# Paired heads, an output product by chunks, a token table by expert, and unread products on TensorE in an encoder layer

## The chip, the cores and the metric

The kernel runs on one core of a Trainium2 chip. The metric is device time of one execution in microseconds (us). Three executions of the kernel before took 1742.06, 1747.69 and 1747.76 us; their median is 1747.69 us. In the profile PE is the matrix engine (PEld its weight loads), DVE the vector engine, ACT the scalar engine, POOL the general engine that also issues indirect transfers, and SP the engine that issues most of the others.

## The reference

One encoder layer on 512 tokens of width 1024, all in float32, written for depth 1:

```python
proj = h @ w_in                      # A: q,k,v  B: q,k,v  C: q,k,v  and three gates
oa = windowed_gqa_sink(...)          # 8 heads, window of 128 each way, sink logit
ob = diff_attention(...)             # 4 heads, softmax1 - lam * softmax2
oc = neighbourhood_attention(...)    # 8 heads on an 8 x 64 grid
merged = sum(sigmoid(gate_i) * (branch_i @ w_branch_i))
x = layer_norm(alpha * x + merged @ w_out)
logits = x @ w_router + b_router     # top 4 of 32 experts, softmax over the 4
y = act(x @ w_up[e] + b_up[e]) @ w_down[e] + b_down[e]     # clamped SwiGLU
x = layer_norm(alpha * x + weighted sum of y over the token's experts)
```

The weights of the 32 experts are 32 x (1024 x 2048 + 1024 x 1024) floats, 384 MB in transfers of 1 MB.

## The kernel before

**Numbers.** A float32 operand is split into a rounded part (`whi`, `vh`, `ph`, suffix h) and a remainder (suffix l), both of the type fp32r, ACT making the first and DVE the second. A product is then three matmuls: h·h, l·h and h·l. Experts of the kind L are computed so for up to 128 tokens, experts of the kind S in plain float32 for up to 64, in the order of the string `KINDS` (16 of each, L and S mostly in turn).

**Attention.** `proj` (L126) makes a projection for 128 columns in 24 matmuls. `banded` (L230) does one head of A or C: for each of four blocks of 128 queries `scores` (L198) makes two matmuls, L203 over 128 rows (both parts of q against the rounded k) and L204 over the head's 64 rows (the remainder of k), and `soft` (L207) adds the bias, finds the maximum and takes the exponential into a tile `E`. Then the probabilities are turned on PE (L260), split (`split_pt`) and multiplied with v by `pv3` (L225): L226 `vh·ph`, L227 `vl·ph`, L228 `vh·pl`, each with 64 output rows. The two heads of a pair are done one after the other. `att_b` does the same for B with 512 keys per block and 128 output rows. `Fill` takes the next projections and the gated branch products (`ph2_items`) as filler between these steps. A list scheduler then sets the order on each engine.

**The middle.** After the last branch product, `w_out` comes in eight chunks of 512 KB (L792), is split (L793, L794), and `out_product` (L778) makes the output product: for the token chunks c = 0, 1, 2 together, k by k, then for c = 3. `layer_norm1` (L723) follows for each chunk: residual sum (L729), turning on PE (L737), statistics, router logits (L748), the top four and the mask `M`. After c = 3 come the positions of all tokens in their experts (L816 to L823), a one-hot of expert 0's tokens and the gathering of their rows on PE (L835, four chunks), the split of these rows (`xt0`), and `finish1` of all four chunks, which writes X1 and Y.

**The experts.** `weights` (L1052) hands out the stream of 1 MB weight tiles. Eight tiles hold raw weights: `rawu` (four) and `rawv` (four), filled by SP (L610 up, L615 down) as they come free. An L tile comes free when ACT and DVE have split it (L1064, L1065) into a ring of three; an S tile when PE has used it. The first eight are expert 0's; whose weights come next is in `order`, which `sort` (L888) computes while `up(0)` (L1071) has begun. `table` (L910) writes a token's place into T in DRAM with 16 indirect transfers on POOL (L933), in the sorted order of the experts, and reads the table back; `pick` (L1019) on POOL copies the columns that put an expert's bias on PE. Expert 1, of the kind S, starts with `pick` and `gather_small`. From expert 6 on `overflow` tests once whether any expert has too many tokens.

Of the kernel before, what the change touches and what calls it, by code (L numbers as in the profile page):

```python
# [23 lines left out]
P = 128  # L24
S = 512
# [18 lines left out]
def kernel_body(ctx, tc, a, out, dbg=None, cap=128):  # L44
# [56 lines left out]
    for k in range(8):  # L101
        t = att.tile([P, NB, P], F32, name="E", bufs=7) if k < 7 else att.tile([P, NB, P], F32, name="t", bufs=3)
# [66 lines left out]
    def make_v(w, permuted, box):  # L169
# [8 lines left out]
        vh = att.tile([P, NB, P], F32R, name="vh", bufs=2)  # L178
        vl = att.tile([P, NB, P], F32R, name="vl", bufs=2)
# [3 lines left out]
        nc.scalar.copy(vh, pt)  # L183
        nc.vector.tensor_sub(vl, pt, vh.bitcast(F32))
        box["v"] = (vh, vl)
# [12 lines left out]
    def scores(box, u, qb, ks, ke):  # L198
        q2, (k2, kl) = box["q"], box["k"]
        r = slice(u * 64, u * 64 + 64)  # L200
        qs = slice(qb * P, qb * P + P)
        ps = ps_s.tile([P, S], F32, name="sc")
        nc.tensor.matmul(ps[:, :ke - ks], q2[:, u, qs], k2[:, u, ks:ke], start=True, stop=False)  # L203
        nc.tensor.matmul(ps[:, :ke - ks], q2[r, u, qs], kl[r, ks:ke], start=False, stop=True)  # L204
        return ps[:, :ke - ks]

    def soft(ps, bias, n, init, mcol, scol):  # L207
# [3 lines left out]
        e = att.tile([P, S], F32, name="E", bufs=7)  # L211
# [18 lines left out]
    def banded(box, u, biasf, init, sinkc, done):  # L230
        vh, vl = box["v"]
        vc = slice(u * 64, u * 64 + 64)
        m = att.tile([P, NB], F32, name="m", bufs=4)
        s = att.tile([P, NB], F32, name="s", bufs=4)
        es = []
        for qb in range(NB):
            ks, ke = rng(qb)
            ps = scores(box, u, qb, ks, ke)
            es.append(soft(ps, biasf(qb), ke - ks, init, m[:, qb:qb + 1], s[:, qb:qb + 1]))
            yield  # L240
        if sinkc is not None:
            sk = att.tile([P, NB], F32, name="sk", bufs=2)
            nc.scalar.activation(sk, m, AF.Exp, bias=sinkc)
            nc.vector.tensor_add(s, s, sk)
        r = att.tile([P, NB], F32, name="r", bufs=4)
        nc.vector.reciprocal(r, s)
        for qb in range(NB):
            ks, ke = rng(qb)
            nc.vector.tensor_scalar(es[qb][:, :ke - ks], es[qb][:, :ke - ks], r[:, qb:qb + 1], None,
                                    op0=ALU.mult)  # L250
        yield
        po = ps_o.tile([P, S], F32, name="o")
        pend = None
        for i, kb in enumerate((1, 2, 0, 3)):
            qs = [qb for qb in range(NB) if abs(qb - kb) <= 1]
            pt = ps_t.tile([P, S], F32, name="pt")
            n = len(qs) * P
            for j, qb in enumerate(qs):
                c0 = kb * P - rng(qb)[0]
                nc.tensor.transpose(pt[:, j * P:(j + 1) * P], es[qb][:, c0:c0 + P], ident)  # L260
            ph, pl = split_pt(pt, n)
            if pend:
                pv3(*pend)
            pend = (po[:64, qs[0] * P:qs[0] * P + n], n, ph, pl, vh[:, kb, vc], vl[:, kb, vc], i == 0, i == 3)
            yield
        pv3(*pend)
        done(po[:64])
        yield
# [4 lines left out]
    def evac_o(po, br, half, permuted):  # L273
        bh, bl = br
        r = slice(half * 64, half * 64 + 64)
        hi, hf, lo, src = bh[r], bh[r].bitcast(F32), bl[r], po
        if permuted:
            hi, hf, lo = perm(hi), perm(hf), perm(lo)
            src = out4(src)
        if half == 0:  # L280
# [1219 lines left out]
```

## Time and profile before

| what | value |
|---|---|
| median of three executions | 1747.69 us |
| the profiled execution | 1744.16 us |
| its span (first to last instruction) | 1742.3 us |
| PE busy | 1611.0 us, 92% |
| DVE busy | 940.0 us, 54% |
| ACT busy | 778.3 us, 45% |
| POOL busy | 207.1 us, 12% |
| mean granted clock of PE | 0.975 of 2.4 GHz |
| read from DRAM | 466.78 MB, 278 GB/s over the span |

Busy time of PE counts a matmul from its start to a modelled end, and matmuls overlap, so a PE that is "busy" for a whole stretch can be streaming or only draining. How far apart the starts of two matmuls are says more. The granted clock of a stretch is given as a share of 2.4 GHz. The profile's page cuts the span into 40 slices: up to about 550 us PE is busy and the transfers are light (60 to 80 GB/s), from 700 us to 1714 us both are near full (about 400 GB/s), and between the two neither is.

### The profile page before, as it was taken

Reading aid. Unit: us, or ns where it says so; the run is one execution under the profiler, and the core shown is the slowest. Engines: PE = TensorE matmul, PEld = TensorE weight load, DVE = VectorE, ACT = ScalarE, POOL = GpSimd, SP = SyncE. Lnnn points to the kernel's source line nnn. Section 1 sums busy time; section 2 is a strip of 40 time slices with the busy share of each in tenths; the row PEclk is TensorE's granted clock in tenths of the full one; section 3 lists DMA queues with packets and bytes.
Section 4 is the critical chain, followed back from the end, with each engine's and each line's share of the span. In section 5 each row is a group of like instructions: output and inputs, shape, how many; then the busy total and the mean of one; then the engine's idle time right before and its main releaser. Section 6 shows DMA issues by size and latency. Waiting matters only on the chain.

```text
span 1742.3 us, 19860 instructions
## 1 busy us (share of the span) xinstructions
PE 1611.0 (92%) x7130; PEld 1053.7 (60%) x7130; DVE 940.0 (54%) x1340; ACT 778.3 (45%) x994; POOL 207.1 (12%) x247
## 2 busy tenths in 40 slices
PE   7999999999996966999899999999999999999994
PEld 5677777777785753455375466556546654664541
DVE  4875566555643375355274377536536753664424
ACT  4654545444432342345154266535535653453432
POOL 0000011212101016101012000110100011101000
PEclk9999999999998988999999999999999999999998
DMA  8212222222254164999899999999999999999994
GB/s 200 60 50 66 83 78 77 73 69 76 61 162 161 41 242 185 408 412 401 335 409 411 403 403 385 391 392 410 402 399 395 369 382 394 403 403 406 396 402 193
DMA packets 169208, 478.64 MB, mean 275 GB/s; under 512 B 24441, under 2 KB 94105, under 8 KB 136336
## 3 DMA queue, kind: packets, MB, share of 16 engines
q1 hardware_dynamic: 153648, 452.95, 66.9%
q0 software_dynamic: 8432, 16.21, 3.7%
q10 hardware_dynamic: 7024, 8.16, 1.6%
q8 instruction: 58, 0.95, 0.2%
q14 instruction: 46, 0.38, 0.1%
HBM read 466.78 MB, written 18.40 MB: 278 GB/s over the span
## 4 chain that ended last, share of the span: by engine, by line
PE 38%; DMA 5%; DVE 4%; ACT 3%; issue 1%; DVEq 0%; ACTq 0%
PE h L1084 15%; PE h L1102 7%; PE d L1151 7%; PE d L1166 6%; DVE wlo L1065 3%; DMA rawv<-in_w_down_dram 2%; ACT whi L1064 2%; DMA rawu<-in_w_down_dram 2%; DMA rawv<-in_w_up_dram 1%; PE x L1135 1%; PE x L1014 1%; PE h L1095 0%; ACT yoL L1181 0%; PE h L1079 0%; DVE whi L1413 0%
## 5 line engine op out<-in xcount | busy, mean ns | idle before, releaser
L1065 DVE TENSOR_TENSOR wlo<-rawv,whi 128x2048 fp32r<-128x2048 f32 x104 | 235.1, 2288 | 53.3 <-ACT whi L1064 41.6
L1084 PE MATMUL h<-whi,t 128*128 128x512 f32 x960 | 246.6, 399 | 9.0 <-ACT whi L1064 8.1
L1065 DVE TENSOR_TENSOR wlo<-rawu,whi 128x2048 fp32r<-128x2048 f32 x88 | 199.3, 2288 | 60.5 <-ACT whi L1064 60.1
L1064 ACT CAST whi<-rawv 128x2048 fp32r<-128x2048 f32 x104 | 197.0, 1912 | 55.0 <-DMA rawv<-in_w_down_dram 18.5
L1084 PEld LDWEIGHTS h<-whi,t 128*128 128x128 f32 x960 | 181.3, 190 | 57.3 <-ACT whi L1064 14.9
L1064 ACT CAST whi<-rawu 128x2048 fp32r<-128x2048 f32 x88 | 165.8, 1909 | 37.2 <-DMA rawu<-in_w_up_dram 17.1
L129 PE MATMUL mm<-xh,whi 128*128 128x512 f32 x432 | 178.0, 412 | 0.0
L130 PE MATMUL mm<-xl,whi 128*128 128x512 f32 x432 | 171.8, 398 | 0.0
L131 PE MATMUL mm<-xh,wlo 128*128 128x512 f32 x432 | 171.7, 397 | 0.0
L1114 ACT ACTIVATE sg<-h 128x512 f32<-128x512 f32 x48 | 28.7, 597 | 272.7 <-PE h L1102 152.2
L1151 PE MATMUL d<-whi,t 128*128 128x512 f32 x512 | 143.1, 401 | 2.9 <-ACT whi L1064 2.9
L1084 PE MATMUL h<-wlo,t 128*128 128x512 f32 x480 | 134.8, 402 | 2.2 <-DVE wlo L1065 2.1
L1102 PE MATMUL h<-rawu,xs 128*64 128x512 f32 x512 | 118.6, 603 | 3.6 <-DMA rawu<-in_w_up_dram 3.5
L1102 PE MATMUL h<-rawv,xs 128*64 128x512 f32 x512 | 117.8, 606 | 2.4 <-DMA rawv<-in_w_up_dram 2.4
L71 DVE TENSOR_TENSOR wlo<-raw,whi 128x1024 fp32r<-128x1024 f32 (+1 forms) x78 | 86.2, 1107 | 53.1 <-ACT whi L70 52.5
L1151 PEld LDWEIGHTS d<-whi,t 128*128 128x128 f32 x512 | 96.2, 191 | 27.1 <-ACT whi L1064 4.3
L1115 DVE TENSOR_SCALAR aS<-h 128x512 f32<-128x512 f32 x16 | 11.0, 690 | 187.3 <-PE h L1102 187.3
L1084 PEld LDWEIGHTS h<-wlo,t 128*128 128x128 f32 x480 | 88.9, 190 | 37.4 <-issue 9.7
L70 ACT CAST whi<-raw 128x1024 fp32r<-128x1024 f32 (+1 forms) x78 | 71.3, 915 | 77.2 <-PE mm L130 33.5
L1151 PE MATMUL d<-wlo,t 128*128 128x512 f32 x256 | 84.3, 411 | 14.8 <-DVE wlo L1065 14.7
L129 PEld LDWEIGHTS mm<-xh,whi 128*128 128x128 f32 x432 | 82.3, 190 | 23.0 <-issue 7.6
L212 ACT ACTIVATE E<-t,m 128x256 f32<-128x256 f32 (+2 forms) x96 | 59.1, 616 | 76.5 <-DVE m L210 71.8
(345 smaller groups left out, 2287.7 us busy)
## 6 DMA issues: line engine op xcount, KB each, us to landing
rawu<-in_w_up_dram SPq DMA_DIRECT2D x128, 1024.0 KB, 15.1
rawv<-in_w_up_dram SPq DMA_DIRECT2D x128, 1024.0 KB, 15.7
rawu<-in_w_down_dram SPq DMA_DIRECT2D x64, 1024.0 KB, 15.0
rawv<-in_w_down_dram SPq DMA_DIRECT2D x64, 1024.0 KB, 14.0
raw<-in_w_in_dram SPq DMA_DIRECT2D x50, 512.0 KB, 3.9
raw<-in_w_branch_dram SPq DMA_DIRECT2D x24, 256.0 KB, 2.8
raw<-in_w_out_dram SPq DMA_DIRECT2D x8, 512.0 KB, 5.8
raw<-in_w_in_dram SPq DMA_DIRECT2D x8, 256.0 KB, 4.7
```

The costliest lines, as they stand in the source:

```text
L70: nc.scalar.copy(h, raw)
L71: nc.vector.tensor_sub(l, raw, h.bitcast(F32))
L129: nc.tensor.matmul(ps, wv[0][:, k], xh[:, k], start=(k == 0), stop=False)
L130: nc.tensor.matmul(ps, wv[0][:, k], xl[:, k], start=False, stop=False)
L131: nc.tensor.matmul(ps, wv[1][:, k], xh[:, k], start=False, stop=(k == 7))
L212: nc.scalar.activation(e[:, :n], t[:, :n], AF.Exp, bias=mcol, scale=-1.0, accum_out=scol)
L1064: nc.scalar.copy(h, raw)
L1065: nc.vector.tensor_sub(l, raw, h.bitcast(F32))
L1084: nc.tensor.matmul(hs[n], x_[:, k], w_[:, n // 2, n % 2 * S:(n % 2 + 1) * S], start=False, stop=(last and k == 7))
L1102: nc.tensor.matmul(hs[b][n * 64:(n + 1) * 64], x_, w[:, b, n * S:(n + 1) * S], start=False, stop=(k == 7), skip_group_check=True)
L1151: nc.tensor.matmul(ys[n], x_[:, k], w_[:, j, n * S:(n + 1) * S], start=(k == 0 and i == 0), stop=(k == 7 and i == 2))
L1166: nc.tensor.matmul(ys[m * 64:(m + 1) * 64], x_, w[:, j, n * S:(n + 1) * S], start=(k == 0), stop=(k == 7), skip_group_check=True)
```

## The change

The kernel after differs in these parts.

1. `banded` takes both heads of a pair: `scores` issues the two L203 of a block first and the two 64-row matmuls behind them. The tiles `E` go from 7 to 8. `make_v` puts vh and vl of a head side by side, and the value product is two matmuls: one over 128 output rows (vh and vl against `ph`) and one over 64 (`vh·pl`). `evac_o` adds the two halves (one more copy on ACT for the first head of a pair and one more addition on DVE for every head).
2. Two chunks of `w_out` are read during the last branch products, three more into the memory that comes free behind them; `wo0` lies where the branch tiles of B were.
3. The output product goes chunk by chunk, c = 0 to 3. The layer norm, the positions, the table entries, the gathering for expert 0 and `finish1` of a chunk are done between the products of the next one.
4. Behind chunk 3, the first weight tile of expert 0 is split early (`ready_first`), the counts and the sorted order are made inside the chain, and `keep` puts 2, 3, 9 and 8 matmuls of 512 columns on PE whose results nothing reads.
5. T is laid out by expert, without the sorted order. Twelve of its 16 indirect transfers are issued during the products of chunk 3, four behind the chain. One transfer brings T back as rows of experts, and six matmuls with the permutation put it in the sorted order (`table`), inside `up(0)`. `pick` stands ahead of the last four indirect transfers, and ACT makes `sel`.
6. `gates_all` multiplies the masks that are kept (`mk`), and the expert's number is read on SP behind the transfer before it.

```diff
-    def scores(box, u, qb, ks, ke):
+    def scores(box, qb, ks, ke):
...
+        pss = [ps_s.tile([P, S], F32, name="sc")[:, :ke - ks] for _ in range(2)]
+        for u in range(2):
+            nc.tensor.matmul(pss[u], q2[:, u, qs], k2[:, u, ks:ke], start=True, stop=False)
+        for u in range(2):
+            r = slice(u * 64, u * 64 + 64)
+            nc.tensor.matmul(pss[u], q2[r, u, qs], kl[r, ks:ke], start=False, stop=True)
+        return pss
...
+            def pv(cs, n, kb, ph, pl, first, last):
+                nc.tensor.matmul(po[:, cs], v2[:, kb, u], ph[:, :n], start=first, stop=False, skip_group_check=True)
+                nc.tensor.matmul(po[:64, cs], v2[:, kb, u, :64], pl[:, :n], start=False, stop=last,
+                                 skip_group_check=True)
...
+        t = att.tile([P, S], F32, name="w", bufs=4)
+        nc.scalar.copy(t[r], po[64:])
+        nc.vector.tensor_add(t[r], po[:64], t[r])
...
+    for c in range(NB):
         pss[c] = [ps_y.tile([P, S], F32, name="y") for _ in range(2)]
...
+        for k in range(8):
+            if c == 0:
...
+                nc.scalar.copy(wo[k][:, 0], wos[k])
+                nc.vector.tensor_sub(wo[k][:, 1], wos[k], wo[k][:, 0].bitcast(F32))
...
+            out_product(c, k)
+            if k in (1, 2, 4, 5, 7):
+                stage()
+            if c == NB - 1 and k == 6:
+                stage()
+                gates(range(NB - 1))
...
+    def keep(n):
+
+        with tc.issue_after(chain.pop("pe").ins):
+            if not idle:
+                idle.append(ps_y.tile([P, S], F32, name="y"))
+            for _ in range(n):
+                nc.tensor.matmul(idle[0], bu[:, 0, :P], bu[:, 0], start=True, stop=True)
+
+    last_ = behind(c, ready_first)
+    next(last_)
+    while queue:
+        stage()
+    keep(2)
+    next(last_)
+    keep(3)
+    next(last_)
+    keep(9)
+    next(last_)
+    counts()
+    next(last_)
+    keep(8)
+    sort()
...
+    with tc.issue_after(chain["dve"].ins):
+        table_at(c)
+        gates([c])
+        rest_of_sort()
+        finish1(c)
...
+    def table():
+
+        tt = wk.tile([E, P, 2], I32, name="tt", bufs=1)
+        tf = wk.tile([E, P], F32, name="tf", bufs=1)
+        nc.gpsimd.dma_start(tt, T.rearrange("(e s) i -> e s i", s=P))
         for i in range(4):
-            nc.gpsimd.tensor_copy(sel[i * E:(i + 1) * E, i // 2], pm)
+            nc.scalar.copy(sel[i * E:(i + 1) * E, i // 2], perm_)
+        nc.vector.tensor_copy(tf, tt[:, :, 0])
+        pt = ps_x.tile([P, 4, E], F32, name="x")
+        for j, t in ((0, tf), (1, tt[:, :, 1].bitcast(F32))):
+            nc.tensor.matmul(pt[:, j], t, perm_, start=True, stop=True, skip_group_check=True)
...
-    hs = up(0, {0: [gates], 1: [table], 4: [second]})
+    hs = up(0, {1: [table], 4: [second]})
```

Where this moves instructions, the order on the engines shows it. First PE in the attention of C, scores between filler (`sc` is a score, `mm` filler). Before:

```order
L203 MATMUL sc<-k_3391,q_3321 128x384
L204 MATMUL sc<-kl,q_3321 128x384
L129 MATMUL mm<-xh,whi 128x512
L130 MATMUL mm<-xl,whi 128x512
L131 MATMUL mm<-xh,wlo 128x512
```

After:

```order
L208 MATMUL sc<-k_3364,q_3296 128x384 x2
L211 MATMUL sc<-kl,q_3296 128x384 x2
L129 MATMUL mm<-xh,whi 128x512
L130 MATMUL mm<-xl,whi 128x512
L131 MATMUL mm<-xh,wlo 128x512
```

The 64-row matmuls of two heads now stand side by side. Over the whole order this is so for 28 of the 48 pairs (12 of 512 columns in B, 8 of 384 and 8 of 256 in C); in A and at a few places in B the two still stand apart, each behind its own first matmul.

Second POOL from the selection columns of the experts (`sel`, `pick`) to the first rows that are fetched (`xgS`). Before:

```order
L909 CAST sel<-perm 32x32 x4
L1021 CAST pick<-sel 128x128
L933 DMA T<-row,di 4096x2 x16
L990 MEMSET xgS 128x512
L1021 CAST pick<-sel 128x128
L990 MEMSET xgL 128x1024
L990 MEMSET xgS 128x512
L1021 CAST pick<-sel 128x128
L938 DMA tbs<-T 64x64 x2
```

After:

```order
L748 MEMSET sel 128x64
L883 DMA T<-row,di 4096x2 x12
L1177 CAST pick<-sel 128x128
L883 DMA T<-row,di 4096x2 x4
L1079 DMA tt<-T 32x256
L1146 MEMSET xgS 128x512
L1177 CAST pick<-sel 128x128
L1150 DMA xgS<-X_303,tbs 128x512
```

Four transfers and one read stand between the first `pick` and the second, where 16 stood; the casts of `sel` have gone to ACT.

Third DVE behind chunk 3's chain, in the kernel after only (`xt` are expert 0's rows, `wlo` a split of a weight tile, `row` and `di` the entries of T, `tf` the table that came back):

```order
L876 TENSOR_REDUCE gs<-gk 128x1
L1004 TENSOR_TENSOR wlo<-rawu,whi 128x2048
L879 TENSOR_TENSOR gk<-gk,gs 128x4
L1004 TENSOR_TENSOR wlo<-rawu,whi 128x2048
L880 COPY row<-gk 128x4
L1004 TENSOR_TENSOR wlo<-rawu,whi 128x2048
L1004 TENSOR_TENSOR wlo<-rawv,whi 128x2048 x2
L1082 CAST tf<-tt 32x128
L1004 TENSOR_TENSOR wlo<-rawv,whi 128x2048
L1089 TENSOR_SCALAR tbs<-x,half 128x32
```

The last entries of T are ready behind the second of these splits, and the sixth and seventh wait for the table to come back. On PE the six matmuls of the table stand behind the first matmul of the sixth weight tile of `up(0)`.

## Rows read from the trace of the kernel before

**Rows 1.** Busy time by stretch: length, PE, PEld, DVE, ACT, POOL, clock, DMA share, GB/s

```profile
40.00:112.00 72.00, 71.99 (x349) 50.52 (x349) 57.95 (x161) 47.52 (x126) 1.22 (x2) 1.00 0.22 63
112.00:546.00 434.00, 427.18 (x1910) 327.04 (x1907) 242.01 (x493) 196.96 (x384) 56.19 (x63) 0.99 0.26 79
...
614.00:643.00 29.00, 14.04 (x115) 11.92 (x115) 20.25 (x65) 10.72 (x19) 0.38 (x2) 0.76 0.74 290
643.00:667.00 24.00, 23.31 (x95) 18.84 (x96) 23.87 (x74) 12.90 (x7) 9.98 (x5) 0.93 0.74 291
667.00:691.00 24.00, 10.52 (x37) 3.48 (x38) 9.27 (x37) 3.54 (x5) 19.62 (x25) 0.72 0.19 64
691.00:1714.00 1023.00, 971.06 (x4208) 573.82 (x4206) 521.22 (x368) 458.57 (x383) 110.02 (x93) 0.99 1.00 395
```

**Rows 2.** Timeline of SP, first transfers past expert 0's: start, length, line

```profile
646.35 6.59 SPq L610 DMA_DIRECT2D rawu<-in_w_up_dram  x4
...
691.21 6.25 SPq L615 DMA_DIRECT2D rawu<-in_w_down_dram  x4
```

**Rows 3.** Timeline of PE, scores of B: start, length, line, out<-in, size

```profile
112.51 0.40 PE L203 MATMUL sc<-k,q 128*128 128x512 f32 x1
112.83 0.50 PE L204 MATMUL sc<-kl,q 64*128 64x512 f32 x1
113.27 0.49 PE L203 MATMUL sc<-k,q 128*128 128x512 f32 x1
```

**Rows 4.** Timeline of PE, two matmuls of 64 rows on different halves

```profile
730.98 0.49 PE L1079 MATMUL h<-bu,sel 64*128 64x512 f32 x2
731.41 1.94 PE L1102 MATMUL h<-rawu,xs 128*64 128x512 f32 x8
```

**Rows 5.** Timeline of PE, value products of one key block in A

```profile
103.44 0.42 PE L226 MATMUL o<-ph,vh 128*64 128x384 f32 x1
103.70 0.34 PE L227 MATMUL o<-ph,vl 128*64 128x384 f32 x1
103.88 0.34 PE L228 MATMUL o<-pl,vh 128*64 128x384 f32 x1
104.05 0.38 PE L260 MATMUL pt<-ident,E 128*128 128x128 f32 x2
```

**Rows 6.** Timelines of PE and ACT where the output product begins

```profile
557.53 0.77 PE L783 MATMUL y<-wo,mx 128*128 128x512 f32 x1 [11.73 <-ACT wo L793]
...
561.54 0.80 PE L785 MATMUL y<-wo,mx 128*128 128x512 f32 x1 [2.81 <-DVE wo L794]
...
556.39 2.00 ACT L793 CAST wo<-raw 128x1024 fp32r<-128x1024 f32 x2 [5.33 <-DMA raw<-in_w_out_dram]
```

**Rows 7.** Timeline of PE from the last output product to `up(0)`

```profile
613.75 0.40 PE L785 MATMUL y<-wo,mx 128*128 128x512 f32 x1
...
626.93 0.19 PE L816 MATMUL r<-ones,M 128*32 128x1 f16 x1 [8.51 <-DVE M L763]
...
628.36 9.61 PE L835 MATMUL y<-oh,mx 128*128 128x128 f32 x64 [0.83 <-DVE oh L833]
...
643.24 3.67 PE L1084 MATMUL h<-whi,xt 128*128 128x512 f32 x8
```

**Rows 8.** Timelines of POOL and PE where expert 1 starts

```profile
684.98 0.97 POOL L933 DMA_INDIRECT T<-row,di  x1 [0.30 <-issue]
...
686.40 0.31 POOL L1021 CAST pick<-sel 128x128 fp32r<-128x128 f32 x1
...
686.77 0.79 PE L1095 MATMUL h<-bu,pick 128*128 128x512 f32 x1 [13.29 <-POOL pick L1021]
```

**Rows 9.** The page's costliest groups, a split of expert weights; its DMA issues, Y's rows

```profile
L1065 DVE TENSOR_TENSOR wlo<-rawu,whi 128x2048 fp32r<-128x2048 f32 x88 | 199.3, 2288 | 60.5 <-ACT whi L1064 60.1
...
Y<-yoL,tbl POOLq DMA_INDIRECT x16, 10.3
```

**Rows 10.** One tile's view, T: transfers on POOL with their ns, idle before, landing us

```profile
L933 POOL DMA_INDIRECT T<-row,di x16: 971/972/2867, 663.9 to 685.0; - x16
...
  issue: 4.6, 15
...
DMA to landing us min/median/max: 2.1/2.1/3.0
```

More of the change, by code (lines that the diff above doesn't have):

```diff
@@ L247, in banded @@
[L247 to L264, printed above, removed]
+            pss = scores(box, qb, ks, ke)
@@ L588, in kernel_body, with out_raw @@
     wsp[0] = sW.enter_context(tc.tile_pool(name="wsp", bufs=2))
+    s3 = ExitStack()
+    wraw = s3.enter_context(tc.tile_pool(name="wraw", bufs=2, side="right"))
+    wos = {}
+    def out_raw(k, pool, after=None, **kw):
+        wos[k] = pool.tile([P, D], F32, name="raw", **kw)
+        with ExitStack() as order_:
+            if after is not None:
+                order_.enter_context(tc.issue_after(after.ins))
+            dma(wos[k], a["w_out"][k * P:(k + 1) * P, :])
     nraw = [0]
@@ L696, in put_bu, with bu_load @@
+    burs = []
+    def bu_load():
+        for i in range(2):
+            bur = p3a.tile([P, 2, S], F32, name="xt", bufs=2)
+            dma(bur[:E], a["b_up"].rearrange("e (b n c) -> e n b c", b=2, n=2)[:, i])
+            burs.append(bur)
     def put_bu():
@@ new lines, in sort, with rest_of_sort @@
+    def sort():
+        po = ps_r.tile([1, E], F32, name="r")
+        nc.tensor.matmul(po, pcol[:E], perm_, start=True, stop=True)
+        pd = ps_r.tile([P, 2, E], F32, name="r")
+        nc.tensor.matmul(pd, ones1[:E], dg_, start=True, stop=True)
+        nc.vector.tensor_copy(order, po)
+        nc.vector.tensor_scalar(capr, pd[:, 0], float(NL), cap / 2.0, op0=ALU.is_lt, op1=ALU.mult)
+        nc.vector.tensor_copy(place, pd[:, 1])
+    def rest_of_sort():
+        nc.vector.tensor_scalar(capr, capr, cap / 2.0, None, op0=ALU.add)
+        nc.vector.tensor_sub(cntr, cntr, capr)
+        nc.vector.tensor_scalar(over, cntr, 0.0, None, op0=ALU.max)
+        nc.vector.tensor_reduce(most, cntr, AX.X, ALU.max)
+        nc.vector.tensor_scalar(mxc, most, 0.0, None, op0=ALU.max)
@@ L837, in kernel_body @@
[L837 to L844 removed]
+    ring = ctx.enter_context(tc.tile_pool(name="ringw", bufs=3))
@@ new lines, in chunks, with ready @@
+    def chunks():
+        for p in range(E + 1):
+            if p < E:
+                for k in range(8):
+                    yield KINDS[p], (p == 0 and pre.get(("u", k))) or up_raw(p, k)
+            if p:
+                for t in range(4):
+                    yield KINDS[p - 1], (p == 1 and pre.get(("d", t))) or down_raw(p - 1, t)
+    stream, ahead = chunks(), deque()
+    def ready():
+        kind, raw = next(stream, ("", None))
+        if raw is None:
+            return False
+        raw = raw.rearrange("p (j c) -> p j c", j=2)
+        if kind == "L":
+            h, l = (ring.tile([P, 2, D], F32R, name=n) for n in ("whi", "wlo"))
+            with ExitStack() as order_:
+                for e in chain.values():
+                    order_.enter_context(tc.issue_after(e.ins))
+                nc.scalar.copy(h, raw)
+                nc.vector.tensor_sub(l, raw, h.bitcast(F32))
+            raw = h, l
+        ahead.append((kind, raw))
+        return True
@@ new lines, in ready_first @@
+    def ready_first(held):
+        chain.clear()
+        chain["dve"] = held
+        ready()
+    idle = []
+    def keep(n):
[7 more added lines that the diff above has]
+    while queue:
+        stage()
+    keep(2)
+    next(last_)
@@ L1304, in kernel_body @@
     idxs[0]["xt"] = xt0
-    sort()
     def second():
```

546 lines of the change are left out of this document (277 added, 269 removed).

## The prediction

> **What bounds the kernel now.** I read the stretches first [rows 1]. From 112 to 546 us PE is busy 427.18 of 434 us, DVE 242.01, and DMA has a share of 0.26: PE sets the pace there, so time taken off PE comes off the end. From 40 to 112 us PE is full too, but DVE has 57.95 of 72 us. From 691 to 1714 us DMA is at 1.00 and 395 GB/s: the weights of experts 1 to 31 set the pace, whatever PE does. Between the two nothing is full: from 614 to 643 us PE is busy 14.04 of 29 us at a clock of 0.76, and from 667 to 691 us DMA has a share of 0.19.
>
> Why DMA rests there shows on SP [rows 2]: at 646.35 it issues tiles into the first buffers that expert 0 frees, and with eight buffers of 1 MB it then has none until 691.21, when expert 1 gives some back. Expert 1's first matmul starts at 686.77, after PE waited 13.29 us for `pick`, which stands on POOL behind the transfers to T [rows 8]. So SP resumes 4.44 us after expert 1 starts, the full stretch takes 1023 us, and 28 us follow to the end of the span. **The time is the start of expert 1 plus a block that the change does not touch.** What has to be summed is the way to 686.77: attention, the seam to the output product (11.73 and 2.81 us idle before its first matmuls [rows 6]), chunk 3's chain (from 613.75 to 643.24 [rows 7]) and `up(0)` (43.5 us from there to 686.77).
>
> **The change, part by part.** The sum is made against the profiled execution, 1744.16 us, which lies 3.5 under the median.
>
> *Scores.* In B the full matmul starts 0.32 us before the 64-row one, and that one 0.44 before the next full one [rows 3]. Column by column, 384 columns stream in 0.175 us [rows 5], hence 512 in 0.233 and 256 in 0.117. So entering the 64-row form costs 0.09 and leaving it 0.21. Two 64-row matmuls on different halves took 0.43 us from the first start to the next full one [rows 4], as long as one: they run side by side. A pair set side by side therefore saves one stream and one switch (0.30): 0.53, 0.48 and 0.42 us. With 12, 8 and 8 such pairs that is 6.4 + 3.8 + 3.4 = 13.6 us, all in the stretch that PE fills. The pairs that stay apart save nothing.
>
> *Value products.* One of three matmuls goes, 0.175 us at 384 columns and 0.117 at 256; a head has two blocks of each: 0.58 us. The eight heads of C give 4.7. Those of A I count as nothing: DVE is at 80% there and gets an addition per head, 0.57 us by a quarter of the split of 2048 columns in 2288 ns [rows 9], an estimate; ends 0 and 4.7. ACT's added copy, about 0.5 us by the casts of 1024 columns in 1.0 us [rows 6], lies beside PE. Sum of attention: **-18 us**, between 0 (DVE or the E tiles bind) and -24 (A gains too).
>
> These value products now alternate between 128 and 64 output rows. In the rows the entry into 64 output rows costs 0.26 less 0.175, 0.085 us, and leaving is free (0.17 to the next start) [rows 5]; a block pays that once now and once then, so I add nothing. The Trainium skill (TensorEngine Tiling (Array Packing), section Key Properties) says that changing the tiling mode, not just the tile, drains TensorE; [rows 3] agree with it, and the free way back in [rows 5] does not. If a change back cost here what it costs in the scores, 0.21 us, 64 blocks would pay 13.4 us; that is a rival below.
>
> *Seam.* From the end of the last branch product (557.53 - 11.73 = 545.8 [rows 6]) to the end of the last output product (613.75 + 0.40 [rows 7]) it takes 68.35 us: 15.75 to the first l·h product, then 52.6 of products. Two chunks of `w_out` now come in earlier and the others into memory that is free; the first wait becomes one cast and one split after the last branch copy, about 5 us (ends 2 and 11.7). The 52.6 us stay (the same products in another order). Into them go three quarters of the gathering of expert 0's rows, 7.2 of 9.61 us at a clock of 0.76 [rows 1, 7], 5.5 at full clock, say 5, and the chunk-wise stages, whose PE parts are small and whose DVE parts lie beside the products. 5 + 52.6 + 5 is 62.6: **-6 us**, ends 0 and -9. SP takes over some loads from ACT's queue; they are small and early, so nothing.
>
> *Chain of chunk 3.* It takes 29.1 us now. Three quarters of the gathering go (-7.2). The 8.51 us wait for M [rows 7] holds DVE work of the earlier chunks; I take 5 of it off (ends 0 and 8.5). From the gathering's end (637.97) to 643.24 lie 5.3 us with the sort's matmuls and the split of the rows; the sort is now made in gaps, about half, -2.8. **-15 us**, ends -7 and -18. Into this chain come the early split of a weight tile (2.29 us on DVE [rows 9], placed in DVE's waits for PE and ACT) and 22 unread products, 22 x 0.233 = 5.1 us on PE, which is idle 15 of 29 us there. They stand ahead of whatever PE gets next, so one that is late costs at most its own group (9 x 0.233 = 2.1); I take 0. What they can give back is the clock: the first eight matmuls of `up(0)` take 3.67 us [rows 7], 0.46 each, twice 0.233. This is the lower level, 1.2 GHz, after a stretch with PE half idle.
>
> *`up(0)`.* Without its wait it is 43.5 - 13.3 = 30.2 us, 3.8 per tile. `pick` now stands ahead of the last four transfers, so the wait for it goes. What is late next is the table, which PE needs at the sixth tile. Call the start of `up(0)` U. DVE first does chunk 3's entries, masks and `finish1` (some 5 us of small operations, an estimate) and two splits of 2.29: entries ready at U+10. Then four transfers on POOL, of 0.97 us and 0.30 between them [rows 10], 5.1 us; 2.1 to 3.0 until the last has landed; the read back about as long again; a cast: U+22. The sixth split waits on DVE behind that cast and the other splits behind it; PE is held with it: 22 + 2.3 + 3 x 3.8 = U+36 in place of U+43.5. **-8 us**, ends -14 (the table costs no wait) and +8 (each of the two landings takes the 10.3 us of Y's rows [rows 9] in place of 2.1, which is 16 more). Chunk 3's rows of X1 and Y now go out on SP between tiles of expert 1; those buffers come free later than the issue, so nothing.
>
> **Sum:** -18 - 6 - 15 - 8 = -47 us: 1697.2 by the profiled execution, 1700.7 by the median. **I forecast 1699 us**, with 1682 to 1712 as the range of this case.
>
> **Rivals.** *Attention gains nothing* (0.12): the eight `E` tiles are exactly one pair's, so the next pair's scores wait for turned blocks, and DVE has the more work. For it: 80% of DVE in A. Against: from 112 us on DVE has 56%, and filler stands between. 1699 + 18 = 1717.
>
> *The table comes back late* (0.10): landing as Y's rows do. For it: the weight stream fills the DMA queues at the same time (0.74 from 643 us on). Against: T's own landings were 2.1 to 3.0 in that state [rows 10]. 1699 + 16 = 1715.
>
> *The unread products do not hold the clock, or do so and delay the chain* (0.03): half clock over the first tile or two, or one group late: +2 to +5, 1703.
>
> *Each change back from 64 output rows drains PE* (0.03), for 13.4 us: 1712. Against: [rows 5], where it is free.
>
> *Slower* (0.07, of which 0.05 past the point): the pairs run in lockstep. With both heads of a pair in flight and as many `E` tiles as one pair fills, PE can run out of filler and wait for the maximum, the exponential and the turning of each pair. Eight pairs of A and C; attention's gain is gone (1717), and each pair costs x: 1717 + 8x passes 1756 from x = 5 us on, and a pair of A takes 18 us now (72 us for four). For it: the ring holds no block of the next pair in reserve. Against: the filler still stands between the scores, and PE's own share leaves nothing to wait for before. At x = 7 it is 1773.
>
> **How the numbers follow.** The forecast's case has 0.65 (1682 to 1712); the rivals 0.12, 0.10, 0.03, 0.03 and 0.07. The range goes from 1680 to 1724: it holds most of the forecast's case, the single mishaps at 1703 to 1717, and their sums in part; lockstep beyond 1 us a pair and two large mishaps together, about 0.15 with the far ends of the sum, stay out. About 0.5%, 9 us, is what a measurement of this kernel can tell from no change. Faster by more than that: all cases but lockstep, 0.93; within it (lockstep with x of 3 to 5 us) 0.02; slower 0.05.
>
> **What would show it.** Right: the last branch product ends about 528 us in place of 546; the wait for `w_out` is about 5 in place of 14.5 us; from the last output product to `up(0)` some 14 us at a clock near 1; no wait for `pick`, but one of some 6 us in `up(0)` that ends with the table or a split behind it; expert 1 starts near 640 and the full stretch still takes 1023 us. Wrong: PE with idle time for `E`, `pt` or DVE in attention (lockstep); a wait for the table over 10 us; a chain over 20 us; or a full stretch that grows, which would say that the block is not fixed.

## The result and the profile after

Four executions of the changed kernel took 1711.30, 1716.77, 1718.38 and 1722.41 us, median 1717.58, against 1746.88 us before: a ratio of 0.984 [0.982, 0.986], 29 us less. The forecast was 1699. The profiled execution took 1711.30 us, 32.9 less than that of before.

Busy time by stretch, in the columns of [rows 1] (attention in two parts, chunk 3's chain, `up(0)`, the weight stream):

```profile
40.00:112.00 72.00, 69.86 (x314) 47.84 (x314) 58.37 (x161) 49.09 (x127) 2.14 (x2) 0.98 0.17 52
112.00:533.00 421.00, 406.58 (x1873) 319.23 (x1872) 245.50 (x508) 197.73 (x389) 56.30 (x62) 0.99 0.28 85
599.00:612.00 13.00, 11.10 (x76) 7.64 (x75) 9.58 (x37) 8.96 (x18) 10.26 (x10) 1.00 0.99 313
612.00:654.00 42.00, 32.76 (x128) 23.60 (x128) 23.28 (x51) 16.30 (x12) 15.85 (x12) 0.84 0.65 230
658.00:1682.00 1024.00, 973.62 (x4211) 575.20 (x4209) 522.96 (x376) 457.64 (x383) 100.63 (x90) 0.99 1.00 395
```

The stretch with DMA at 1.00 is as long as before, and the chain is now 13 us at full clock. But PE, which was busy 427.18 of 434 us in attention, is now busy 406.58 of 421: idle time there has grown from 6.8 to 14.4 us. And `up(0)` still takes 42 us, 9 of them without PE.

The places that answer to [rows 6, 7, 8], from the timeline of PE: the first output product, the first of `up(0)`, and what PE does around the table:

```profile
536.21 0.77 PE L835 MATMUL y<-wo,mx 128*128 128x512 f32 x1 [3.49 <-DMA ln<-in_ln_g_dram]
536.77 0.63 PE L836 MATMUL y<-wo,mx 128*128 128x512 f32 x1
537.20 0.63 PE L835 MATMUL y<-wo,mx 128*128 128x512 f32 x1
...
542.09 0.40 PE L835 MATMUL y<-wo,mx 128*128 128x512 f32 x1
542.33 0.39 PE L836 MATMUL y<-wo,mx 128*128 128x512 f32 x1
...
611.87 2.14 PE L1216 MATMUL h<-whi,xt 128*128 128x512 f32 x8
...
629.59 0.39 PE L1216 MATMUL h<-whi,xt 128*128 128x512 f32 x1
636.96 0.60 PE L1085 MATMUL x<-perm__4862,tf 32*128 32x32 f32 x2 [6.98 <-issue]
...
654.42 0.47 PE L1227 MATMUL h<-bu,pick 128*128 128x512 f32 x1 [0.64 <-DVE aL L1247]
```

Marks of the two profiles, each the start of a row or its start plus length (expert 1 by its first weight product, 0.4 to 0.7 us behind the row that the prediction used):

| step | before | after | moved | forecast |
|---|---|---|---|---|
| to the end of the last branch product | 545.80 | 532.72 | -13.1 | -18 |
| from there to the end of the last output product | 68.35 | 65.62 | -2.7 | -6 |
| from there to `up(0)` | 29.09 | 13.53 | -15.6 | -15 |
| from there to expert 1 | 44.26 | 42.95 | -1.3 | -8 |
| from there to SP's next transfer | 3.71 | 3.40 | -0.3 | 0 |
| from there to the end of the span | 1051.09 | 1051.28 | +0.2 | 0 |

So 14 of the 47 us forecast are missing in these two profiles (18 by the medians), most of them in attention and in `up(0)`. Attention has two stages: A and B from the first score of all (38.70 us before, 37.48 after) to the first score of C (288.17 and 279.81), and C from there to the mark. A and B took 249.5 us before and 242.3 after, 7.1 less where the forecast has 6.4 (the pairs of B). C took 257.6 and 252.9, 4.7 less where the forecast has 11.9 (7.2 for its pairs and 4.7 for its value products). The remaining 1.2 us of the first mark lie before the first score. So what is missing in attention is missing in C.

Two stretches show where it went, 100 to 150 us (A ends, B begins) and 290 to 460 us (C). Idle time is the length less PE's busy time; what a low clock takes is the length times what lacks to 1.00. Before:

```profile
100.00:150.00 50.00, 49.30 (x226) 37.14 (x226) 33.28 (x97) 24.11 (x53) 2.89 (x4) 0.93 0.20 59
...
290.00:460.00 170.00, 164.61 (x758) 126.84 (x757) 96.48 (x179) 77.60 (x154) 33.56 (x34) 1.00 0.26 74
```

After:

```profile
100.00:150.00 50.00, 45.75 (x215) 33.90 (x214) 39.90 (x106) 24.01 (x53) 3.21 (x3) 0.97 0.32 91
...
290.00:460.00 170.00, 159.44 (x745) 125.49 (x744) 98.32 (x198) 80.63 (x166) 34.97 (x35) 0.98 0.25 71
```

In C 5.4 us of idle time became 10.6, and the clock takes 3.4 more. At the end of A 0.7 us of idle time became 4.2, while the clock took 3.5 us before and 1.5 after. The timelines say why in C (POOL, ACT and PE of the kernel after; the same happens again at 418 us):

```profile
364.47 2.70 POOL L404 TENSOR_TENSOR bias<-cm,craw 128x256 f32<-128x256 f32 x2 [12.63 <-DVE m L217]
...
367.92 0.73 POOL L404 TENSOR_TENSOR bias<-cm,craw 128x256 f32<-128x256 f32 x1
```

```profile
368.68 0.33 ACTq L401 DMA_DIRECT2D craw<-in_na_rpb_dram  x1
369.06 0.58 ACT L164 CAST k<-mm 64x512 fp32r<-64x512 f32 x1 [3.34 <-POOL bias L404]
```

```profile
370.86 0.33 PE L275 MATMUL pt<-ident,E 128*128 128x128 f32 x1 [2.14 <-DVE E L258]
...
371.77 0.63 PE L129 MATMUL mm<-xh,whi 128*128 128x512 f32 x1
372.20 0.63 PE L130 MATMUL mm<-xl,whi 128*128 128x512 f32 x1
```

Both bias tiles of a pair are in use until both heads have their scores, so POOL makes the next pair's first bias late. `craw` is one tile, so the load of the second one waits for POOL, and it is issued by ACT: the cast of `k` stands behind it for 3.34 us, then the remainder on DVE, then the scaling of the probabilities, and PE rests 2.14 us. Behind that its matmuls start 0.43 us apart, at 1.2 GHz.

At the end of A, ACT, POOL and PE:

```profile
101.69 0.58 ACT L292 COPY w<-o 64x512 f32<-64x512 f32 x1 [1.28 <-PE o L266]
...
104.17 0.58 ACT L164 CAST k<-mm 64x512 fp32r<-64x512 f32 x1
```

```profile
104.81 1.53 POOL L166 CAST k<-k 64x512 fp32r<-64x512 f32 x1 [10.18 <-ACT k L164]
```

```profile
106.39 0.50 PE L208 MATMUL sc<-k,q 128*128 128x512 f32 x1 [1.78 <-POOL k L166]
...
118.09 0.33 PE L266 MATMUL o<-pl,v 128*64 128x256 f32 x1 [1.01 <-DVE pl L229]
```

The copy at 101.69 is an added one. It stands in ACT's queue ahead of the first keys of B, and PE waits for these and, for the last heads of A, for the addition and the remainders on DVE. (The list of changes gives one more copy to the first head of a pair. That holds in C. In A both heads of the first and of the third pair get one; those of the other two pairs had theirs before.) The kernel before lost time here too, behind a copy of its own (ACT and PE):

```profile
119.38 0.58 ACT L286 COPY w<-o 64x512 f32<-64x512 f32 x1 [0.68 <-PE o L228]
119.99 0.58 ACT L176 COPY w<-mm 128x512 f32<-128x512 f32 x1
...
120.62 0.81 PE L182 MATMUL mm<-ident,w 128*128 128x128 f32 x4 [0.62 <-ACT w L176]
```

Last, the table, on POOL:

```profile
621.45 2.77 POOL L883 DMA_INDIRECT T<-row,di  x1 [2.58 <-DVE row L880]
624.53 1.89 POOL L883 DMA_INDIRECT T<-row,di  x1 [0.30 <-issue]
626.72 1.90 POOL L883 DMA_INDIRECT T<-row,di  x1 [0.30 <-issue]
628.92 0.98 POOL L883 DMA_INDIRECT T<-row,di  x1 [0.30 <-issue]
634.68 0.59 POOL L1079 DMA_DIRECT2D tt<-T  x1 [4.77 <-DMA T<-row,di]
```

The transfers begin 9.6 us after `up(0)` has begun, the four take 8.45 us in place of 5.1, the last lands 4.8 us behind, and the table is on PE at 636.96, 25.1 us after the start of `up(0)`.

### The profile page after: what moved, and what is told of

Same layout as the page of the kernel before. It is cut to its first block, busy times and chain, and to the rows that moved or that the text cites. A ratio compares the mean times of both kernels' runs of the same rounds, so it can differ in the third digit from the quotient of the medians.

```text
span 1709.5 us, 19798 instructions
## 1 busy us (share of the span) xinstructions
PE 1596.4 (93%) x7100; PEld 1049.4 (61%) x7100; DVE 941.1 (55%) x1313; ACT 785.3 (46%) x1009; POOL 202.2 (12%) x243
## 4 chain that ended last, share of the span: by engine, by line
PE 39%; DVE 5%; ACT 4%; DMA 4%; issue 1%; DVEq 0%; ACTq 0%
PE h L1216 15%; PE d L1283 8%; PE h L1234 8%; PE d L1298 6%; DVE wlo L1004 3%; ACT whi L1003 3%; DMA rawv<-in_w_down_dram 2%; DMA rawu<-in_w_down_dram 2%; PE x L1267 1%; PE x L1170 1%; ACT yoL L1313 1%; PE h L1227 0%; PE h L1211 0%; DVE whi L1547 0%; PE x L1421 0%
## 5 line engine op out<-in xcount | busy, mean ns | idle before, releaser
L131 PEld LDWEIGHTS mm<-xh,wlo 128*128 128x128 f32 x432 | 81.4, 188 | 17.5 <-issue 0.6
## 6 DMA issues: line engine op xcount, KB each, us to landing
rawu<-in_w_down_dram SPq DMA_DIRECT2D x64, 1024.0 KB, 14.8
```

Source lines behind the costliest of these rows:

```text
L131: nc.tensor.matmul(ps, wv[1][:, k], xh[:, k], start=False, stop=(k == 7))
```

## Experiments

Marks and stages of every kernel's profile in us, its median time, and idle time and clock loss of the two stretches (100 to 150, 290 to 460) worked out as above. The first mark counts from the start of the program, and the first score of A starts anywhere between 37.5 and 41.7 us in these profiles; the two stages do not hold that difference. The four rows from "after, again" on ran on one chip, the next four on a second, the last four on a third; the kernel before took 1743.2, 1742.9 and 1744.8 us beside them.

| kernel | branch products end | A and B | C | last output product to `up(0)` | `up(0)` to expert 1 | A/B idle, clock | C idle, clock | median us |
|---|---|---|---|---|---|---|---|---|
| before | 545.80 | 249.5 | 257.6 | 29.1 | 44.3 | 0.7, 3.5 | 5.4, 0 | 1746.88 |
| after | 532.72 | 242.3 | 252.9 | 13.5 | 43.0 | 4.2, 1.5 | 10.6, 3.4 | 1717.58 |
| after, again | 538.28 | 245.4 | 254.4 | 16.7 | 43.7 | 4.4, 5.0 | 10.2, 5.1 | 1720.73 |
| craw on POOL | 527.43 | 245.3 | 242.7 | 17.6 | 42.5 | 4.9, 3.5 | 3.5, 0 | 1712.40 |
| table later | 535.29 | 245.1 | 252.4 | 16.2 | 33.2 | 3.0, 7.0 | 10.0, 3.4 | 1711.79 |
| both edits | 533.27 | 251.4 | 242.7 | 17.8 | 30.1 | 3.0, 13.5 | 3.7, 0 | 1706.13 |
| both, no pairs | 540.71 | 252.0 | 249.5 | 13.5 | 32.0 | 4.8, 3.5 | 2.3, 0 | 1710.72 |
| both, three products | 524.39 | 237.1 | 245.5 | 13.5 | 31.7 | 0, 0 | 1.8, 0 | 1694.44 |
| no unread products | 540.97 | 248.3 | 253.7 | 15.7 | 43.1 | 2.6, 12.0 | 11.2, 3.4 | 1725.51 |
| both, no unread | 528.26 | 246.5 | 242.6 | 14.8 | 31.1 | 4.0, 7.0 | 3.4, 0 | 1699.77 |
| three products | 533.83 | 237.2 | 257.9 | 13.5 | 42.6 | 0, 0 | 9.8, 5.1 | 1711.18 |
| both, three in A only | 519.03 | 237.2 | 242.6 | 13.5 | 32.0 | 0, 0 | 3.5, 0 | 1691.27 |
| both, three, no unread | 523.42 | 237.2 | 245.4 | 14.8 | 30.5 | 0, 0 | 1.8, 0 | 1692.82 |
| both, three, again | 523.43 | 237.2 | 245.4 | 13.5 | 32.1 | 0, 0 | 1.9, 0 | 1694.77 |

### The two new waits, each taken away

The kernel after, unchanged:

> The kernel after once more, unchanged, as the base for the other three of this batch. By its first profile: the last branch product ends near 533 us, up(0) begins near 612, expert 1 near 654. The four times shown of it lie between 1711 and 1722 us; if a run has something of its own, the marks of the profile show in which stretch.

1720.73 us, 0.988 [0.986, 0.990] of before. Its profile is 8.6 us longer than the first, most of it in two places: A and B take 3.1 us more (5.0 us of clock in place of 1.5 where A ends), and 3.1 us more pass before `up(0)`, where PE waits 2.75 us for nothing that the profile names. Its first score starts 0.9 us later, and C takes 1.5 more.

```diff
-            nc.scalar.dma_start(raw, rp[h])
+            nc.gpsimd.dma_start(raw, rp[h])
```

> One edit: the eight loads of the bias rows of C's heads (craw) are issued by POOL instead of ACT; the order on PE is the same. My theory: C gained little because ACT stands 2.6 to 3.3 us behind POOL's first bias of a pair (3 times) before it can issue the second load, so k, its remainder on DVE and the scaled probabilities come late and PE waits 2.14 us twice and runs at half clock behind it. Then ACT's wait for POOL bias (12.6 us in all in C) goes, PE's waits of 2.1 us for E go, and the last branch product ends 4 to 7 us earlier than in the kernel after (near 527). Rival: with two heads in flight the scaled probabilities are late of themselves (DVE has the work of eight blocks at once); then the waits for E stay at 1.5 us or more each and the end moves by less than 2 us.

1712.40 us, 0.984 [0.982, 0.986], 8.3 less than the kernel after in the same batch. PE in C:

```profile
290.00:460.00 170.00, 166.51 (x795) 131.23 (x794) 100.73 (x206) 86.78 (x176) 38.21 (x40) 1.00 0.26 74
```

PE's waits for E in C fell from 6.4 to 1.7 us and the clock stays at 1.00, with the same order on PE. The theory holds; the scaled probabilities were late because of ACT's queue. By the stage the wait is worth more than the 4 to 7 us expected: C takes 252.4 to 254.4 us in the four profiles with the merged product and the load on ACT, and 242.6 or 242.7 in the four with the load on POOL, so some 10 to 12 us.

```diff
-        for i in range(4):
-            nc.scalar.copy(sel[i * E:(i + 1) * E, i // 2], perm_)
-        nc.vector.tensor_copy(tf, tt[:, :, 0])
+        with tc.issue_after(last["oh"].ins):
+            nc.vector.tensor_copy(tf, tt[:, :, 0])
...
-    hs = up(0, {1: [table], 4: [second]})
+    hs = up(0, {1: [sels], 4: [second], 7: [table]})
```

(`last["oh"]` is the last one-hot of expert 1's rows; `sels` holds the four copies of `sel` that stood in `table`.)

> The table comes later: its cast on DVE is put behind the one-hots of expert 1's rows and its six matmuls on PE behind the last tile of up(0). My theory: expert 1 waits in the kernel after because the sixth and later splits and PE stand behind the table (7.0 us of PE, then a tile at half clock). Then from up(0) to expert 1's first product 33 to 36 us pass in place of 42.6, and the time falls by 6 to 9 us. Rival: something else holds expert 1's start (the gathering of its rows, or the last tiles of expert 0, which come late); then PE waits in another place and the stretch stays over 40 us, the time within 2 us.

1711.79 us, 0.983 [0.981, 0.984], 8.9 less than the kernel after beside it. Expert 1 starts 33.2 us after `up(0)`, in place of 43.7 beside it. The table's matmuls now come where nothing waits for them:

```profile
646.59 1.08 PE L1215 MATMUL h<-wlo,xt 128*128 128x512 f32 x4
647.80 0.37 PE L1084 MATMUL x<-perm__4862,tf 32*128 32x32 f32 x2
...
649.36 1.07 PE L1233 MATMUL h<-rawu,xs 128*64 128x512 f32 x2
```

So the wait for the table, the splits behind it and the low clock after it cost about 10 us of `up(0)`. The edit moves the cast on DVE and the matmuls on PE together; what each is worth alone was not tried.

> Both edits together. If both theories hold and the two places are in series, the savings add: 10 to 16 us less than the kernel after, 1701 to 1708 us by its median of 1717.6. If one of the rivals holds, only the other's part is seen. If the start of the weight stream is bound elsewhere (by what SP issues), the gain before expert 1 is seen in the marks but not in the end.

1706.13 us, 0.977 [0.976, 0.979]: 14.6 less than the kernel after, near the sum of the two (17.3). In its profile the clock where A ends takes 13.5 us, more than in any other, which hides the gain in C at the first mark (C itself takes 242.7 us, as with `craw` on POOL).

### The parts of attention, each undone

```diff
         for u in range(2):
             nc.tensor.matmul(pss[u], q2[:, u, qs], k2[:, u, ks:ke], start=True, stop=False)
-        for u in range(2):
             r = slice(u * 64, u * 64 + 64)
```

> The kernel with both edits (craw on POOL, the table later), and scores issued per head again: each 64-row matmul stands behind its own first one. It undoes the pairing alone. By the starts in the first profile of the kernel after, the scores of all pairs take 53.8 us there and 63.4 before, 9.6 less; the prediction had 13.6. My theory: PE is what is short, and the last branch product ends 9 to 14 us later than with both edits (533.3 there, with the clock low for a while between 110 and 145 us, which can move it by some 10 us and is to be taken off with the clock of that stretch). Rival: the pairing's gain is given back as waits for the other engines; then undoing it costs under 4 us.

The time alone, 1710.72 against 1706.13 us, is within what the clock at the end of A moves. The stages tell more beside the kernel with `craw` on POOL, which has the same attention but for the pairs and, in its profile, the same clock loss there, 3.5 us: A and B take 252.0 against 245.3 us, C 249.5 against 242.7. By these two profiles the pairing is worth 6.7 and 6.8 us, 13.4 together; the prediction had 6.4 for B and 7.2 for C, 13.6. (The starts of the scores alone, in the expectation, account for 9.6.)

```diff
-                nc.tensor.matmul(po[:, cs], v2[:, kb, u], ph[:, :n], start=first, stop=False, skip_group_check=True)
-                nc.tensor.matmul(po[:64, cs], v2[:, kb, u, :64], pl[:, :n], start=False, stop=last,
-                                 skip_group_check=True)
+                pv3(po[:64, cs], n, ph, pl, v2[:, kb, u, :64], v2[:, kb, u, 64:], first, last)
...
-        nc.scalar.copy(t[r], po[64:])
-        nc.vector.tensor_add(t[r], po[:64], t[r])
-        hi, hf, lo, src = bh[r], bh[r].bitcast(F32), bl[r], t[r]
+        hi, hf, lo, src = bh[r], bh[r].bitcast(F32), bl[r], po[:64]
```

> The kernel with both edits, and the value product as three matmuls of 64 output rows again, with no addition of halves (16 copies on ACT, 16 additions on DVE less). It undoes the merged value product alone. By the starts, value products took 36.5 us before and 30.3 after: 6.2. My theory: 5 to 9 us later at the last branch product, part of it in A too. Rival from the prediction: nothing in A, as DVE is at 80% there and has the additions; then the stretch from 40 to 110 us takes the same, and the sum is under 5 us. Second rival: each change back from 64 output rows drains PE in the merged form; then three matmuls cost nothing more or less than two.

1694.44 us, 11.7 less than with the merged product: my theory and both rivals fall, since none had the undoing as a gain. By the stages A and B take 14.3 us less and C 2.9 more; another 4.3 us of the difference lie before `up(0)`, where the profile of the base has the wait that nothing explains. The edit takes away more than the change had put in: of the 16 copies eight stood in the kernel before. Between 100 and 150 us PE now has neither idle time nor a low clock, in this profile and in the four others with three products in A. Hence the next two. The kernel after with this part alone undone:

> The kernel after with one part undone: the value product as three matmuls of 64 output rows and no addition of halves. With both edits this undoing made the time 11.7 us less by the medians (1694.4 against 1706.1), though the products themselves take 6 us more of PE. My theory now: the added copies and additions stand before the keys of B on ACT, DVE and POOL where A ends, PE rests there 4 us between 100 and 150 us, and its clock falls to the lower level for 2 to 14 us' worth behind it. Then the idle time of that stretch falls under 1 us and its clock loss under 2 us in this kernel too, and the time lies 5 to 12 us under the kernel after (1706 to 1713 against 1717.6 and 1720.7). Rival: the difference came from the chip or the later order, and the merged product is worth its 4.7 us: then this kernel is 3 to 8 us slower than the kernel after.

1711.18 us, 0.981 [0.979, 0.983], 6.4 and 9.6 us under the two medians of the kernel after. The two stretches:

```profile
100.00:150.00 50.00, 49.99 (x260) 39.31 (x259) 37.37 (x102) 25.40 (x55) 3.41 (x4) 1.00 0.28 81
...
290.00:460.00 170.00, 160.24 (x751) 125.71 (x749) 89.83 (x189) 74.68 (x158) 35.23 (x35) 0.97 0.24 68
```

The loss where A ends is gone, that in C (`craw`) is still there: two separate causes. And three products in A alone, with the merged one and its addition kept in C:

> Both edits, three value products in A (no addition of halves there), the merged product in C only. My theory: what the merged product costs, it costs where A ends; in C PE has cover. Then the stretch from 100 to 150 us is as in the kernel with three products everywhere (idle under 1 us, clock loss under 2 us), C gives 2 to 4 us of PE, and the time is 1690 to 1695 us. Rival: the additions cost in C as well (waits for DVE there, E and pl); then it is 1696 to 1702.

1691.27 us, 0.969 [0.967, 0.972], the lowest median of all, 26 us under the kernel after (its five executions, 1686.6 to 1696.5 us, overlap those of the kernels with three products everywhere):

```profile
100.00:150.00 50.00, 50.00 (x260) 39.27 (x260) 37.28 (x103) 25.33 (x56) 3.40 (x4) 1.00 0.28 81
...
290.00:460.00 170.00, 166.54 (x795) 131.54 (x794) 99.91 (x207) 86.34 (x176) 39.52 (x41) 1.00 0.27 79
```

Its branch products end at 519.03, against 523.43 with three products everywhere in the same batch. But 1.6 of these 4.4 us lie before the first score, where the two kernels are the same. The first score of A and the first of C, with three products in A only, then everywhere:

```profile
39.24 0.35 PE L208 MATMUL sc<-k,q 128*128 128x256 f32 x1
276.44 0.37 PE L208 MATMUL sc<-k,q 128*128 128x256 f32 x1
```

```profile
40.85 0.36 PE L208 MATMUL sc<-k,q 128*128 128x256 f32 x1
278.00 0.36 PE L208 MATMUL sc<-k,q 128*128 128x256 f32 x1
```

From there to the end C takes 242.6 us with the merged product and 245.4 without: it gives 2.8 us, as the theory has it. In A and B it costs 8.2 us beside the kernel with `craw` on POOL (245.3 against 237.2), and 5 to 14 over the seven profiles with pairs that have it there (242.3 to 251.4); the five without it lie between 237.1 and 237.2.

> The kernel with both edits and three value products once more, as the base of this batch. It took 1694.4 us (1689.7 to 1696.5) in its first runs; if the low clock where A ends is gone for good in it, its times stay between 1688 and 1697 and no profile shows a clock loss over 2 us between 100 and 150 us.

1694.77 us, 1693.5 to 1696.0 in five executions: they lie 2.4 us apart, where the first four of the kernel after lay 11 apart.

### The unread products

All three kernels leave out the 22 products whose results nothing reads (`range(n)` made `range(0)`).

> The kernel after without the 22 unread products, the table where the change put it. My theory: the first tiles of up(0) run at the low clock, 2 to 4 us slower, but PE then waits less for the table, which comes at the same time (25 us behind the start of up(0)); expert 1 starts within 1.5 us of the kernel after, counted from the last output product (56.5 and 60.4 us in its two profiles). Rival: the low clock lasts past the table, and all of 2 to 5 us arrives at expert 1.

From the last output product expert 1 comes after 58.9 us, between the 56.5 and 60.4 of the kernel after, as the theory has it. The time, 1725.51 us, is higher. In the profiled execution, 1720.26 us and 9.0 above the first profile of the kernel after, 8.3 of that lie ahead of the output product, long before the first place that the edit touches: the clock takes 12.0 us where A ends. What the slower executions lost is not shown.

> The kernel with both edits and without the 22 unread products. My theory: the first eight matmuls of up(0) then start 0.4 us apart, as before, in place of 0.23 to 0.27, and the low clock lasts for a tile or two: expert 1 starts 2 to 5 us later after the last output product than with both edits (47.9 us there). Rival: the products hold no clock, or delay the chain as much as they give; then the stretch is 47 to 49 us without them too.

The stretch is 45.9 us, less than the 47.9 of its base and nearer the rival; expert 1 does not come later. But this base does not test the clock. Behind the wait before `up(0)` that nothing explains, its own first eight matmuls of `up(0)` take 3.4 us, as they do here without the products. The other profiles tell more: with the products and without that wait the eight take 2.1 us in six of six, with the wait 2.9 to 3.8 in four, without the products 3.4 to 3.8 in three.

> Both edits, three value products, and no unread products. From the last output product to expert 1 the kernels with unread products took 47.9, 45.5 and 45.1 us, the one without them 45.9. My theory: the unread products give nothing that shows: the same stretch is 45 to 48 us and the time 1692 to 1697. Rival: they hold the clock and are worth 2 to 5 us: then 1697 to 1700 us and the stretch is 48 us or more.

1692.82 us (1690.9 to 1696.0) against 1694.77 (1693.5 to 1696.0), 45.3 against 45.5 us. The products hold the clock and shorten the chain (13.5 us against 14.8), but `up(0)` is longer by as much (32.1 against 30.5). In these two profiles something other than PE's clock then sets when expert 1 starts; what it is was not found. The unread products give nothing that can be measured here.

## Why the prediction was right in its direction and too large in its size

**Right.** PE sets attention's pace, the weight stream is a block that only moves, and the time is the start of expert 1 plus that block (1051.1 and 1051.3 us). The pairing was forecast at 13.6 and measured at 13.4 us, the chain at -15 and -15.6. The rival of lockstep, slower than before, did not come: PE was idle for 16.6 us in all of attention from 40 us on, about 2 a pair of A and C, where 5 more a pair were the point. The chain came out by its terms too. On PE after (the end of the router's part, the first work with chunk 3's mask, the gathering):

```profile
602.92 0.33 PE L804 MATMUL y<-ident,ltp 128*128 128x128 f32 x1 [0.23 <-DVE ltp L801]
...
605.79 0.18 PE L846 MATMUL r<-M,lt 128*128 128x32 f16 x1 [0.48 <-DVE M L814]
...
606.78 2.02 PE L852 MATMUL y<-oh,mx 128*128 128x128 f32 x16 [0.28 <-DVE keyr L895]
```

The gathering is 7.6 us shorter (forecast 7.2), from the router to the mask 2.5 us pass in place of 8.5 (6.0 less, forecast 5), and from the gathering to `up(0)` 3.1 in place of 5.3 (2.2 less, forecast 2.8). No run undid the chain or the seam by itself. That the median, 1717.6, is the number of the rival in which attention gains nothing (1717) is chance: attention gained 12 us between its first score and its last branch product.

**The wait that took the place of others in C.** This is the step that failed with the largest price: the 11.9 us that the forecast takes from C, of which 4.7 came in the first profile of the kernel after and 3.2 in the second. The prediction asked what PE's products cost and whether DVE or the ring of E would bind. It did not ask what a pair in flight does to the two bias tiles, though `craw` is issued on ACT's queue in the code. Price: 10 to 12 us by the stage, 8.3 by the medians of one batch. Without this wait C takes 14.9 us less than in the kernel before, more than forecast; the 5.4 us of idle time that the kernel before had there shrink too, to 3.5. The merged product in C, forecast at 4.7, is worth 2.8; PE is idle there for 1.6 us more than with three products (3.5 against 1.9).

**The merged product in A.** The second step that failed is "those of A I count as nothing ... ends 0 and 4.7", although the text had DVE at 80% there. The same paragraph says that ACT's copy "lies beside PE". Measured: 8.2 us lost beside one profile, 5 to 14 over seven. The copies and additions stand in front of what B needs first, and the idle microseconds behind them cost again through the clock. That taking the halves out by a copy and an addition causes it is shown (three products in A: no idle time, no low clock, in five profiles of five); how much of it is the copy and how much the addition was not tried. The kernel with three products also lacks four copies that A had before the change, and the kernel before lost 4.2 us in the same stretch (0.7 idle, 3.5 of clock). Against the kernel before, A and B therefore came out at -7.1 us in the first profile, past the forecast of -6.4, and at -4.1 in the second. That the first met the forecast is luck: its low clock where A ends was short (1.5 us).

**`up(0)`.** The wait was foreseen in its place and kind ("PE is held", some 6 us; measured 6.98), but the term of -8 us was mis-sized: it measured -1.3. The table came at 25.1 us in place of 22, and from there to expert 1 17.5 us passed in place of 13.7, the first of them at half clock. POOL's four transfers alone took 3.4 more than assumed: they run beside DVE's splits, 1.9 to 2.8 us each, and 0.98 for the one that came behind them; before, the first of the 16 ran beside a split and took 2.87, the others 0.97 [rows 10]. The Trainium skill (GPSIMD Engine Reference, section Key points) says that GpSimd shares its SBUF interfaces with VectorE, with contention where an instruction of VectorE has two SBUF inputs. The rows agree in time; no run took the splits away. The rival of late landing holds in part: T's transfers landed after 6.7 us in the median, 2.1 before, while the weights stream beside them.

**The seam.** -6 became -2.7. The wait was 3.5 us, less than the 5 assumed, but from the first output product to the end of the last it took 62.1 us in place of 57.6 (52.6 and 5). The output products start at half clock until about 541.5 us (0.43 us apart, later 0.24), though so did those before (0.43 us apart from 562.1 to 564.7 us), and the stages of a chunk stand between the products on PE in order, with waits of up to 0.9 us each.

**The drain.** The rival that has PE drain at each change back from 64 output rows gave 13.4 us for 64 blocks, 6.7 for the 32 of C: the merged product would have lost 2 us there. It gained 2.8, so the runs show no such price. The Trainium skill (TensorEngine Tiling (Array Packing), section Key Properties) says that changing the tiling mode drains TensorE; these runs do not show it on the way back from 64 output rows.

## What to carry to other kernels

When PE is the bound and some of its work is taken away, look on each other engine's queue at what is put in front of what PE needs next, at every border between phases, and not only at that engine's busy share. When two units of work are put in flight together, list every buffer that both now hold, and on which queue the next fill of it is issued; a load on ACT's queue that waits for a buffer holds ACT's arithmetic. A wait for a table or another late result costs least behind the last thing that does not need it: here six matmuls moved by three tiles were worth 9 us. And compare a stage from its own first instruction: a mark that counts from the start of the program also holds what differs before the stage, here up to 4 us.

## What the runs showed of the hardware that was not expected

After a few idle microseconds at the end of A the clock falls, and how long it stays low differs between kernels with the same order on PE there and between executions of one: over 100 to 150 us it was 0.97 and 0.90 in two profiles of the kernel after, 0.76 without the unread products and 0.73 with both edits. In the kernel before it was 0.93, with 0.7 us of idle time. The longest in detail, 110 to 145 us of the kernel with both edits:

```profile
110.00:145.00 35.00, 34.13 (x114) 26.05 (x115) 22.57 (x69) 12.46 (x27) 0.00 (x0) 0.61 0.19 53
```

So 3 to 5 us of idle time cost 1.5 to 13.5 us more, from one execution to the next, and between the two profiles of the kernel after this makes 3.5 of their 8.6 us. Before `up(0)` PE waits 2.8 to 4.2 us in four profiles, and DVE 3.0 to 3.7, for nothing that the profile names. These are the four profiles of one batch, the kernel after among them; the nine others of changed kernels, on other chips or in another batch, do not have it, and its cause stays open.
